# LayerNorm at a stage boundary of a two-layer hybrid step: the first four products on the raw input, mean and deviation applied on eviction

## The chip, the core and the metric

One core of one Trainium2 chip. The time is device microseconds from the first to the last instruction of one execution; a timed run takes the median of several executions. One further execution was taken by the hardware profiler, and all rows below are from it.

## What is computed

Two layers over 128 context and 256 latent tokens of width 1024. Each layer is FFN, mixer (low-rank attention beside a bidirectional RG-LRU), FFN, each closed by a LayerNorm of the sum with the input:

```
h = x * (1 + m[1]) + m[0]
x = layer_norm(ALPHA * x + 0.5 * m[2] * swiglu(h, w_ffn_up[0], w_ffn_down[0]), ...)
h = x * (1 + m[4]) + m[3]
x = layer_norm(ALPHA * x + m[5] * mixer(h), ...)
h = x * (1 + m[7]) + m[6]
x = layer_norm(ALPHA * x + 0.5 * m[8] * swiglu(h, w_ffn_up[1], w_ffn_down[1]), ...)
```

`swiglu` is silu(h Wg) * (h Wx) times W_down, with a hidden width of 2816. The nine vectors `m` of each layer are silu(cond) @ w_mod, one set for context tokens and one for latent tokens. The mixer's input projection makes four chunks of the recurrence's input (which first goes through a convolution over time, width 4), two of the key/value latent, the rotary key, three query chunks and four gate chunks.

## The kernel before

Activations lie transposed: X is 8 chunks of 128 features by 384 tokens in SBUF, fp32. Every product is done with three matmuls of a split in two halves: `piece` (L306) makes wh (a cast by ACT) and wl (a subtraction by DVE) of a weight block of 128 x 1024, `split_affine` (L275) makes hh and hl of the input, and `mm3` (L319) adds wh*hh + wh*hl + wl*hh into a PSUM tile. Four PSUM buffers ("acc") hold products, three split buffers hold pieces, three staging buffers of 1 MB hold weights that the SP queue loads, and three buffers "t1" of 128 x 384 hold short-lived activations.

A stage boundary is `next_input` (L453): the last chunk of the old stage is added to X (`Residual.add`, L347), the statistics are finished by single-column matmuls on PE (`moments`, L378), DVE subtracts the mean and multiplies by the reciprocal deviation, chunk by chunk (L400, L401; both vectors lie broadcast in PSUM), `split_affine` makes hh and hl of the chunk (ACT for hh; ACT for the fp32 copy of odd chunks and DVE for that of even ones; DVE for hl, L286), and POOL scales X for the next residual (L461). The first product of the new stage needs chunk 0 of hh and hl, and each product needs all eight chunks. There are five such boundaries; the last LayerNorm has its own class.

The vectors `m` are computed beside all this by a `Pump` of 64 steps, each with a load of w_mod (1 MB in one or two transfers) into one of three buffers. Vector steps run on DVE in the up stages of two FFNs; tensor steps are matmuls on PE (L238, tile "gm"). Where they stand is set by hand:

```
UP = [f for f in range(3, 21) if f % 3]
PLAN = ((UP, ()), (UP, ()), ((), ()), ((), ()))
NEXT_STEPS = (3, 3, 4, 3, 3)
MIX_STEPS = (14, 10)
```

NEXT_STEPS are run at the five boundaries, MIX_STEPS behind each mixer's attention. A framework puts each engine's instructions in a static order before the run: by program order among those that it reckons ready. So a step that stands late in the program fills holes in the work before it. Each engine then goes through its list in order.

Of the kernel before, what the change touches and what calls it, by code (L numbers as in the profile page):

```python
# [9 lines left out]
F32 = mybir.dt.float32  # L10
# [59 lines left out]
PLAN = ((UP, ()), (UP, ()), ((), ()), ((), ()))  # L70
NEXT_STEPS = (3, 3, 4, 3, 3)
MIX_STEPS = (14, 10)
# [3 lines left out]
def hybrid_step_kernel(ctx: ExitStack, tc: tile.TileContext, A):  # L76
# [182 lines left out]
    def h_tiles(name):  # L259
        hh = act.tile([P, KD, T], F32R, tag="hh", name=f"hh_{name}")  # L260
        hl = act.tile([P, KD, T], F32R, tag="hl", name=f"hl_{name}")
        return hh, hl
# [12 lines left out]
    def split_affine(hh, hl, c, G, B):  # L275
# [10 lines left out]
        nc.vector.tensor_tensor(hl[:, c, :], h32, hh[:, c, :].bitcast(F32), op=ALU.subtract)  # L286
# [37 lines left out]
    def product(ps, w, col, hh, hl, nk=KD):  # L324
        wh, wl = piece(w[:, :, col : col + P])
        for k in range(nk):
            mm3(ps, wh[:, k], wl[:, k], hh[:, k, :], hl[:, k, :], k == 0, k == nk - 1)
# [10 lines left out]
    class Residual:  # L338


        broadcast = True

        def __init__(self, name, gate):
            self.name, self.gate = name, gate
            self.sums = [tmp.tile([P, T], F32, tag=f"sum{i}", name=f"sum{i}_{name}", bufs=1) for i in range(2)]

        def add(self, c, ps):  # L347
            last = c == KD - 1
            with tc.high_priority(offset=CHAIN_AHEAD) if last else ExitStack():
                for r, (t0, t1) in enumerate(COND):  # L350
                    nc.vector.scalar_tensor_tensor(X[:, c, t0:t1], ps[:, t0:t1], self.gate[:, c, r : r + 1], X[:, c, t0:t1],  # L351
                                                   op0=ALU.mult, op1=ALU.add)
                sq = self.sums[1]
                if c > 0:
                    sq = tmp.tile([P, T], F32, tag="sq", name=f"sq_{self.name}_{c}", bufs=3)
                nc.scalar.activation(sq, X[:, c, :], AF.Square)
            if c == 0:
                return
# [19 lines left out]
        def moments(self):  # L378

            name = self.name  # L380
            with tc.high_priority(offset=CHAIN_AHEAD):
                self.columns(0, self.tail[0])
                self.columns(1, self.tail[1], stop=True)
                if self.broadcast:
                    nc.tensor.matmul(self.pm[:, :T], mean_w, self.tail[0], start=False, stop=True)
                mv = self.pt[:, :6].rearrange("p (a b) -> p a b", b=2)
                m2 = tmp.tile([P, 4], F32, tag="m2", name=f"m2_{name}")
                nc.scalar.activation(m2[:, :3], mv[:, :, 0], AF.Square)
                nc.vector.scalar_tensor_tensor(m2[:, :3], mv[:, :, 1], LN_EPS, m2[:, :3], op0=ALU.add, op1=ALU.subtract)
                rs = tmp.tile([P, 4], F32, tag="r4", name=f"r_{name}")  # L390
                nc.gpsimd.tensor_tensor(rs[:, :3], m2[:, :3], mhalf[:, :3], op=ALU.pow)
            return mv, rs

        def normalise(self):
            _, rs = self.moments()
            pm, pr = self.pm, misc_tile()
            for i in range(3):
                nc.tensor.matmul(pr[:, i * P : (i + 1) * P], rs[:, i : i + 1].to_broadcast([P, P]), ident, start=True, stop=True)
            for c in range(KD):
                nc.vector.tensor_tensor(X[:, c, :], X[:, c, :], pm[:, :T], op=ALU.subtract)  # L400
                nc.vector.tensor_tensor(X[:, c, :], X[:, c, :], pr[:, :T], op=ALU.mult)  # L401
                yield c

    class LastResidual(Residual):


        broadcast = False

        def __init__(self, name, gate):
# [16 lines left out]
        def finish(self, dsts):  # L426
            mv, rs = self.moments()
# [25 lines left out]
    def next_input(res, l, s, nl, nm, steps):  # L453
        pump.step(steps)
        pump.finish()
        G, B, ag = boundary_vectors(l, s, nl, nm)
        hh, hl = h_tiles(f"{nl}{nm}")
        for c in res.normalise():
            split_affine(hh, hl, c, G, B)
        for c in range(KD):  # L460
            nc.gpsimd.tensor_scalar(X[:, c, :], X[:, c, :], ag[:, 0, c : c + 1], ag[:, 1, c : c + 1],  # L461
                                    op0=ALU.mult, op1=ALU.add)
        return hh, hl


    def ffn(l, s, hh, hl, up_steps, down_steps, opened=(), residual=Residual):
        wu, wd = A["w_ffn_up"][l, s], A["w_ffn_down"][l, s]
        with tc.tile_pool(name=f"ffn{l}{s}", bufs=1) as fp:
# [3 lines left out]
            def gated(f, pg, px):  # L472
                a = tmp.tile([P, T], F32, tag="t1", bufs=3, name=f"a{l}{s}_{f}")
                nc.scalar.activation(a, pg[:, :T], AF.Silu)
                nc.vector.tensor_tensor(a, a, px[:, :T], op=ALU.mult)  # L475
# [6 lines left out]
            while f0 < NF:  # L482
                n = min(2, NF - f0)
                wg, wx = (load_rows(wu, 0, KD, o + P * f0, n * P) for o in (0, DFF))
                for i in range(n):
                    f = f0 + i
                    pg, px = acc_tile(), acc_tile()
                    product(pg[:, :T], wg, i * P, hh, hl)
                    product(px[:, :T], wx, i * P, hh, hl)
                    gated(f, pg, px)  # L490
# [10 lines left out]
            res = residual(f"f{l}{s}", gate)  # L501
# [34 lines left out]
    def mixer(l, hh, hl, steps):  # L536
        w_in = A["w_in"][l]
        with ExitStack() as es:
# [18 lines left out]
            for c in range(NLC):  # L557
                if c % 2 == 0:
                    w = load_rows(w_in, 0, KD, O_UX + c * P, 2 * P)
                ps = acc_tile()  # L560
                product(ps[:, :T], w, (c % 2) * P, hh, hl)
                conv(l, c, us[c], ps)
# [17 lines left out]
            for j in range(2):  # L580
                ps = acc_tile()
                product(ps[:, :T], w, j * P, hh, hl)
# [32 lines left out]
            product(ps[:, :T], w, 0, hh, hl)  # L615
# [15 lines left out]
            for j in range(3):  # L631
# [3 lines left out]
                product(ps[:, :T], w, (j % 2) * P, hh, hl)  # L635
# [15 lines left out]
            def gate_branch(c):  # L651
# [3 lines left out]
                product(ps[:, :T], w_g[0], (c % 2) * P, hh, hl)  # L655
# [75 lines left out]
            mh, ml = h_tiles(f"mix{l}")  # L731
            for c in range(NLC):
                nc.scalar.copy(mh[:, 4 + c, :], us[c])
                nc.vector.tensor_tensor(ml[:, 4 + c, :], us[c], mh[:, 4 + c, :].bitcast(F32), op=ALU.subtract)
# [4 lines left out]
            for hp in range(H // 2):  # L739
# [47 lines left out]
                nc.scalar.copy(mh[:, hp, :], ops[:, :T])  # L787
                nc.vector.tensor_tensor(ml[:, hp, :], ops[:, :T], mh[:, hp, :].bitcast(F32), op=ALU.subtract)
# [4 lines left out]
            res = Residual(f"m{l}", modv[l][:, 5])  # L793
            for j in range(KD // 2):
                w = load_rows(A["w_o"][l], 0, KD, 2 * P * j, 2 * P)
                for i in range(2):
                    ps = acc_tile()
                    wh, wl = piece(w[:, :, i * P : (i + 1) * P])
                    for n, k in enumerate((4, 5, 6, 7, 0, 1, 2, 3)):
                        mm3(ps[:, :T], wh[:, k], wl[:, k],  # L800
                            mh[:, k, :], ml[:, k, :], n == 0, n == KD - 1)
                    res.add(2 * j + i, ps)
        return res

    def conv(l, c, u, ps):
# [6 lines left out]
        nc.scalar.activation(u, ps[:, :T], AF.Identity, bias=vec["conv_b"][:, l * NLC + c : l * NLC + c + 1], scale=wk(2))  # L812
# [206 lines left out]
```

## Time and profile before

| | us |
|---|---|
| median of 3 timed runs | 1606.52 (1605.67 to 1615.58) |
| the profiled execution, its own time | 1607.12 |
| its span, first to last instruction | 1605.3 |
| PE busy | 1552.4 (97%) |
| DVE busy | 949.3 (59%) |
| ACT busy | 660.5 (41%) |
| POOL busy | 161.0 (10%) |

Matmuls overlap one another, so a busy PE can still be slow. In each stretch the count of product matmuls says how much of the stage's work was done. The profile shows the TensorE clock as a share of 2.4 GHz.

A row of the windows below has the window (us from the span's start), its length, then busy us and count of instructions of PE, weight loads, DVE, ACT and POOL in this order (with only one tile's instructions, the engines that touch it), then the granted clock, the busy share of the DMA engines and GB/s. Rows of groups by line have the line, engine, operation, out<-in with shapes and count, then busy us and the mean ns of one.

### The profile page before, as it was taken

The page shows a single profiled execution, that of the slowest core. Times are in us where ns is not written, and L with a number is a line of the kernel's source. Part 1 is how long each engine was busy: PE and PEld are TensorE (multiplying, and loading weights), DVE is VectorE, ACT ScalarE, POOL GpSimd, SP SyncE. Part 2 cuts the span into 40 slices and gives each one's busy share as a digit, 9 for nine tenths or more (in the row PEclk, how much of TensorE's full clock was granted, in tenths as well). Part 3 has the DMA queues.
Part 4 walks back from the last instruction along what each step waited for, and adds up shares of the span by engine and source line. Part 5 has one row for each costly group of instructions (what it writes and reads, how often), then busy time and mean ns, then how long its engine had stood idle before and what let it go on. Part 6 is the DMA issues. An engine that isn't in the chain of part 4 may idle for free.

```text
span 1605.3 us, 22927 instructions
## 1 busy us (share of the span) xinstructions
PE 1552.4 (97%) x9234; PEld 1448.7 (90%) x9234; DVE 949.3 (59%) x1568; ACT 660.5 (41%) x1068; POOL 161.0 (10%) x142
## 2 busy tenths in 40 slices
PE   6999999999999999999999999999999989999997
PEld 5899999987668899999989999997867789999996
DVE  3778754477986946863474444345788664444334
ACT  3533323268743533332253333234775444333321
POOL 0000002220004100001220000032000240000011
PEclk9999999999999999999999999999999989999998
DMA  8866563346644535563454343334565214433331
GB/s 295 278 215 203 173 202 133 116 151 209 226 166 157 184 117 199 184 203 119 134 183 150 106 137 119 128 107 157 152 193 197 79 53 131 142 121 128 121 118 40
DMA packets 214790, 249.93 MB, mean 156 GB/s; under 512 B 26394, under 2 KB 193308, under 8 KB 211612
## 3 DMA queue, kind: packets, MB, share of 16 engines
q1 hardware_dynamic: 214684, 248.47, 46.6%
q8 instruction: 72, 1.18, 0.3%
q14 instruction: 34, 0.28, 0.1%
HBM read 245.52 MB, written 1.88 MB: 154 GB/s over the span
## 4 chain that ended last, share of the span: by engine, by line
PE 87%; DVE 5%; issue 3%; DMA 2%; ACT 2%; POOL 1%; SPq 0%; DVEq 0%; POOLq 0%; ACTq 0%
PE acc L320 26%; PE acc L321 26%; PE acc L322 26%; PE gm L238 2%; DVE wl L316 1%; PE acc L753 1%; DMA wm<-in_w_mod_dram 1%; PE ms L375 1%; PE pv L786 1%; DMA ws<-in_w_ffn_up_dram 1%; PE ms L769 1%; ACT wh L315 0%; DVE hl L286 0%; POOL sum_f L361 0%; PE ms L320 0%
## 5 line engine op out<-in xcount | busy, mean ns | idle before, releaser
L315 ACT CAST wh<-ws 128x1024 fp32r<-128x1024 f32 (+1 forms) x332 | 336.2, 1014 | 779.4 <-PE acc L321 545.3
L316 DVE TENSOR_TENSOR wl<-ws,wh 128x1024 fp32r<-128x1024 f32 (+1 forms) x332 | 411.3, 1240 | 382.3 <-ACT wh L315 380.7
L320 PE MATMUL acc<-hh,wh 128*128 128x384 f32 x1280 | 428.6, 339 | 7.9 <-ACT hh L278 7.4
L322 PE MATMUL acc<-hh,wl 128*128 128x384 f32 x1280 | 431.0, 337 | 2.9 <-DVE wl L316 2.9
L321 PE MATMUL acc<-hl,wh 128*128 128x384 f32 x1280 | 431.1, 338 | 1.1 <-DVE hl L286 1.0
L320 PEld LDWEIGHTS acc<-hh,wh 128*128 128x128 f32 x1280 | 241.8, 190 | 15.7 <-ACT hh L278 9.2
L322 PEld LDWEIGHTS acc<-hh,wl 128*128 128x128 f32 x1280 | 241.9, 189 | 8.6 <-DVE wl L316 5.5
L321 PEld LDWEIGHTS acc<-hl,wh 128*128 128x128 f32 x1280 | 241.9, 189 | 8.5 <-DVE hl L286 4.9
L320 PE MATMUL acc<-gh,wh 128*128 128x384 f32 x704 | 236.9, 336 | 0.0
L321 PE MATMUL acc<-gl,wh 128*128 128x384 f32 x704 | 236.4, 336 | 0.0
L322 PE MATMUL acc<-gh,wl 128*128 128x384 f32 x704 | 236.1, 335 | 0.0
L320 PEld LDWEIGHTS acc<-gh,wh 128*128 128x128 f32 x704 | 132.2, 188 | 0.4 <-issue 0.4
L321 PEld LDWEIGHTS acc<-gl,wh 128*128 128x128 f32 x704 | 132.4, 188 | 0.0
L322 PEld LDWEIGHTS acc<-gh,wl 128*128 128x128 f32 x704 | 132.2, 188 | 0.0
L475 DVE TENSOR_TENSOR a<-a,acc 128x384 f32<-128x384 f32 x87 | 48.1, 553 | 123.1 <-PE acc L322 121.4
L252 DVE SCALAR_TENSOR_TENSOR gsum<-wm,sil,gsum 128x512 f32<-128x512 f32 x168 | 120.2, 764 | 0.0
L320 PE MATMUL acc<-hh_in,wh 128*128 128x384 f32 x336 | 111.6, 337 | 5.9 <-ACT hh_in L278 5.9
L321 PE MATMUL acc<-hl_in,wh 128*128 128x384 f32 x336 | 113.9, 339 | 0.0
L322 PE MATMUL acc<-hh_in,wl 128*128 128x384 f32 x336 | 113.9, 339 | 0.0
L360 POOL TENSOR_TENSOR sum_f<-X 128x384 f32<-128x384 f32 x4 | 5.1, 1281 | 841.2 <-DVE X L351 841.2
L320 PEld LDWEIGHTS acc<-hh_in,wh 128*128 128x128 f32 x336 | 62.7, 188 | 7.8 <-ACT hh_in L278 6.8
L238 PE MATMUL gm<-wm,sil 128*32 128x128 f32 (+2 forms) x640 | 62.2, 428 | 3.3 <-DVE G L915 1.2
(268 smaller groups left out, 1750.4 us busy)
## 6 DMA issues: line engine op xcount, KB each, us to landing
ws<-in_w_ffn_up_dram SPq DMA_DIRECT2D x84, 1024.0 KB, 5.1
wm<-in_w_mod_dram SPq DMA_DIRECT2D x56, 1024.0 KB, 6.6
ws<-in_w_ffn_down_dram SPq DMA_DIRECT2D x32, 1024.0 KB, 5.3
wm<-in_w_mod_dram SPq DMA_DIRECT2D x32, 512.0 KB, 4.5
ws<-in_w_ffn_down_dram SPq DMA_DIRECT2D x16, 768.0 KB, 4.5
ws<-in_w_in_dram SPq DMA_DIRECT2D x12, 1024.0 KB, 5.3
ws<-in_w_o_dram SPq DMA_DIRECT2D x8, 1024.0 KB
ws<-in_w_ffn_up_dram SPq DMA_DIRECT2D x8, 384.0 KB, 7.0
```

Of the source, the lines that this page charges most:

```text
L238: nc.tensor.matmul(self.ps[32 * g : 32 * g + 32, :n], lhsT, wv[:, g], start=self.fresh, stop=stop)
L252: nc.vector.scalar_tensor_tensor(self.sum[:, r], wv[:, kk], s, self.sum[:, r], op0=ALU.mult, op1=ALU.add)
L315: nc.scalar.copy(parts[0], src)
L316: nc.vector.tensor_tensor(parts[1], src, parts[0].bitcast(F32), op=ALU.subtract)
L320: nc.tensor.matmul(ps, wh, xh, start=start, stop=False)
L321: nc.tensor.matmul(ps, wh, xl, start=False, stop=False)
L322: nc.tensor.matmul(ps, wl, xh, start=False, stop=stop)
L375: nc.tensor.matmul(self.pt[:, 2 * i + j : 2 * i + j + 1], src[:, i * P : (i + 1) * P], mean_w[:, 0:1], start=False, stop=stop and i == T / ...
L475: nc.vector.tensor_tensor(a, a, px[:, :T], op=ALU.mult)
L753: nc.tensor.matmul(views[i], qT[hf][0:96, h % 4, q0 : q0 + P], kT[hf][0:96, h % 4, k0:k1], start=True, stop=True)
L769: nc.tensor.transpose(t0[:, (2 * j + i) * P : (2 * j + i + 1) * P], pr_[:, (0, 512)[i] + j * P : (0, 512)[i] + (j + 1) * P], ident)
L786: nc.tensor.matmul(o[:, P:T], v, pTs[e][:, (j - 1) * 256 : j * 256], start=(j == 1), stop=(j == 3))
```

## The change

The boundary is taken apart. While the old stage still runs, each finished chunk of X is scaled by G = (1 + m) * ln_g and split without LayerNorm (`split_raw`). The first four products of the new stage take these raw halves, and 4 extra columns behind the 384 tokens (-G and B, for context and latent), so that the products of the weights with -G and with B come out in columns 384 to 387 of the same PSUM tile. The four products run in two halves of four input chunks each (`by_half`). Statistics are put behind the second job of the first half, the broadcast deviation behind the fourth; mean and deviation are copied from PSUM to SBUF. On eviction `settle` adds mean times column and multiplies by the deviation. X is centred in `centre`; `normalise` does the multiplication, the split and the scaling on POOL for chunks 0 to 3 behind the first half, for chunks 4 to 7 behind the second. hh and hl are now one pair of tiles for the whole kernel. No pump steps stand at boundaries: 20 and 16 stand behind the two attentions, four in the up stage of the second layer's first FFN.

```diff
-PLAN = ((UP, ()), (UP, ()), ((), ()), ((), ()))
-NEXT_STEPS = (3, 3, 4, 3, 3)
-MIX_STEPS = (14, 10)
+PLAN = ((UP, ()), (UP, ()), ((6, 9, 12, 15), ()), ((), ()))
+MIX_STEPS = (20, 16)
+EXT = T + 4
+    def split_raw(c, G):
+        h32 = tmp.tile([P, T], F32, tag="t1", bufs=3, name=f"raw_{n_ps[0]}_{c}")
+        for r, (t0, t1) in enumerate(COND):
+            nc.scalar.activation(hh[:, c, t0:t1], X[:, c, t0:t1], AF.Copy, scale=G[:, c, r : r + 1])
+            nc.vector.tensor_scalar_mul(h32[:, t0:t1], X[:, c, t0:t1], G[:, c, r : r + 1])
+        nc.vector.tensor_tensor(hl[:, c, :T], h32, hh[:, c, :T].bitcast(F32), op=ALU.subtract)
+    def by_half(jobs, n, after):
+        for half in range(2):
+            k0 = half * HALF
+            parts = {}
+            for j, (ps, w, i) in enumerate(jobs):
+                if id(w) not in parts:
+                    parts[id(w)] = piece(w[:, k0 : k0 + HALF, :])
...
+                after(half, j)
...
+        def centre(self):
+            self.mean = tmp.tile([P, T], F32, tag="sum0", name=f"mean_{self.name}", bufs=1)
+            nc.scalar.copy(self.mean, self.pm[:, :T])
+            for c in range(KD):
+                nc.vector.tensor_tensor(X[:, c, :], X[:, c, :], self.pm[:, :T], op=ALU.subtract)
...
+        def normalise(self, c):
+            nc.vector.tensor_tensor(X[:, c, :], X[:, c, :], self.rstd, op=ALU.mult)
+            split_affine(c, self.G, self.B)
...
+        def settle(self, dst, ps, name):
+            v = tmp.tile([P, 4], F32, tag="ext", name=f"ext_{name}")
+            nc.vector.tensor_copy(v, ps[:, T:EXT])
+            for r, (t0, t1) in enumerate(COND):
+                nc.vector.scalar_tensor_tensor(dst[:, t0:t1], self.mean[:, t0:t1], v[:, r : r + 1], ps[:, t0:t1],
+                                               op0=ALU.mult, op1=ALU.add)
+            nc.vector.tensor_tensor(dst, dst, self.rstd, op=ALU.mult)
+            return v[:, 2:4]
+        def first(self, jobs, evict):
+            self.extend()
+            def after(half, j):
+                if half == 0:
+                    if j == 1:
+                        self.stats()
+                        self.centre()
+                    elif j == 3:
+                        self.deviation()
+                        for c in range(HALF):
+                            self.normalise(c)
+                else:
+                    evict(j)
+                    if j == 3:
+                        for c in range(HALF, KD):
+                            self.normalise(c)
+            by_half(jobs, EXT, after)
```

In an FFN the four jobs are the gate and the value product of hidden chunks 0 and 1, and hidden chunks 2 and 3 go through `by_half` too, with normalised input. Their eviction settles both products, then applies silu with the column for B as its bias. In the mixer the four jobs are the recurrence's input; each is settled into a t1 buffer, gets its bias from two activations, and goes through the convolution from there:

```diff
+            def settled(c):
+                u = tmp.tile([P, T], F32, tag="t1", bufs=3, name=f"ux{l}{c}")
+                b = prev.settle(u, ps[c], f"u{l}{c}")
+                for r, (t0, t1) in enumerate(COND):
+                    nc.scalar.activation(u[:, t0:t1], u[:, t0:t1], AF.Identity, bias=b[:, r : r + 1])
+                conv(l, c, us[c], u)
```

The last two products of the mixer's output projection are done together in two halves of the input, because hh is read there until the end; their chunks 0 to 5 are split raw only behind these matmuls.

## Rows read from the trace of the kernel before

**Rows 1.** busy time by window, steady FFN stretch and first attention

```profile
830.00:1090.00 260.00, 260.00 (x1501) 259.88 (x1501) 108.27 (x124) 87.66 (x118) 16.62 (x12) 1.00 0.38 125
366.00:490.00 124.00, 120.96 (x684) 87.69 (x683) 103.54 (x215) 79.54 (x159) 5.86 (x7) 1.00 0.61 206
```

**Rows 2.** the windows again, product matmuls alone (tile acc), five boundaries

```profile
315.30:345.30 30.00, 18.20 (x93) 16.72 (x93) 3.31 (x10) 2.01 (x3) 0.94 0.45 159
509.00:545.00 36.00, 22.43 (x109) 19.60 (x109) 1.34 (x4) 0.63 (x2) 0.95 0.31 102
808.80:838.80 30.00, 18.43 (x103) 17.27 (x102) 1.82 (x4) 0.96 (x2) 1.00 0.58 210
1096.00:1126.00 30.00, 16.51 (x84) 15.09 (x84) 2.77 (x8) 2.01 (x3) 0.94 0.44 156
1293.00:1330.00 37.00, 25.64 (x127) 23.84 (x126) 2.37 (x6) 0.87 (x2) 0.86 0.17 57
```

**Rows 3.** the windows again, the pump's instructions alone (tile gm)

```profile
315.30:345.30 30.00, 4.93 (x58) 1.92 (x58) 0.00 (x0) 0.94 0.45 159
509.00:545.00 36.00, 3.81 (x30) 0.84 (x30) 1.19 (x3) 0.95 0.31 102
808.80:838.80 30.00, 4.48 (x64) 2.00 (x64) 0.45 (x1) 1.00 0.58 210
1096.00:1126.00 30.00, 6.48 (x34) 1.15 (x34) 0.00 (x0) 0.94 0.44 156
```

**Rows 4.** the windows again, statistics alone (tile ms), third boundary

```profile
808.80:838.80 30.00, 5.40 (x36) 4.55 (x36) 8.24 (x17) 0.17 (x1) 1.00 0.58 210
```

**Rows 5.** timeline of PE, third and fifth boundary: start, us, [idle before]

```profile
813.83 2.79 PE L238 MATMUL gm<-wm,sil 128*32 128x256 f32 x46
...
1300.82 1.00 PE L375 MATMUL ms<-mean_w,X 128*128 128x1 f32 x6 [0.44 <-DVE X L351]
1304.53 1.65 PE L398 MATMUL ms<-ident,r_m 128*128 128x128 f32 x6 [1.40 <-POOL r_m L391]
1307.84 1.33 PE L320 MATMUL acc<-hh,wh 128*128 128x384 f32 x3 [1.67 <-ACT hh L278]
```

**Rows 6.** groups by line and shape: count, busy us, mean ns

```profile
L316 DVE TENSOR_TENSOR wl<-ws,wh 128x1024 fp32r<-128x1024 f32 x280 | 362.6, 1297 | 272.5 <-ACT wh L315 271.5
L351 DVE SCALAR_TENSOR_TENSOR X<-acc,gate,X 128x256 f32<-128x256 f32 x32 | 15.2, 474 | 0.0
L351 DVE SCALAR_TENSOR_TENSOR X<-acc,gate,X 128x128 f32<-128x128 f32 x32 | 11.2, 351 | 31.0 <-PE acc L322 29.7
L284 DVE TENSOR_SCALAR h<-X,G,B 128x256 f32<-128x256 f32 x20 | 9.0, 452 | 0.0
L284 DVE TENSOR_SCALAR h<-X,G,B 128x128 f32<-128x128 f32 x20 | 7.8, 389 | 0.0
L278 ACT ACTIVATE hh<-X,B,G 128x256 fp32r<-128x256 f32 x40 | 23.5, 587 | 0.0
L278 ACT ACTIVATE hh<-X,B,G 128x128 fp32r<-128x128 f32 x40 | 19.5, 488 | 21.0 <-DVE X L401 20.8
```

**Rows 7.** timeline of DVE and POOL, first boundary

```profile
313.29 2.08 DVE L316 TENSOR_TENSOR wl<-ws,wh 128x1024 fp32r<-128x1024 f32 x1 [0.16 <-ACT wh L315]
314.25 1.98 POOL L361 TENSOR_TENSOR sum_f<-sum_f,sq_f 128x384 f32<-128x384 f32 x1
...
320.70 2.40 DVE L400 TENSOR_TENSOR X<-X,ms 128x384 f32<-128x384 f32 x5
341.68 2.03 DVE L817 SCALAR_TENSOR_TENSOR uc<-acc,small,uc 128x126 f32<-128x126 f32 x6
```

**Rows 8.** one line's instructions: minimum, median and maximum ns

```profile
L401 DVE TENSOR_TENSOR X<-X,ms x40: 514/541/555, 324.0 to 1319.0; 128x384 f32<-128x384 f32 x40
...
L286 DVE TENSOR_TENSOR hl<-h,hh x40: 515/562/885, 326.1 to 1321.5; 128x384 fp32r<-128x384 f32 x40
```

**Rows 9.** the chain that ended last, first attention: start, us

```profile
435.53 4.37 DMA wm<-in_w_mod_dram
```

More of the change, by code (lines that the diff above doesn't have):

```diff
@@ L356, in add @@
                 nc.scalar.activation(sq, X[:, c, :], AF.Square)
+                if c == KD - 1 and self.broadcast:
+                    split_raw(c, self.G)
+            if c < KD - 1 and self.early:
+                split_raw(c, self.G)
             if c == 0:
@@ L376, in columns, with stats @@
                                  start=False, stop=stop and i == T // P - 1)
-        def moments(self):
+        def stats(self):
             name = self.name
[L381 to L392, printed above, removed]
@@ L394, in normalise @@
-        def normalise(self):
-            _, rs = self.moments()
-            pm, pr = self.pm, misc_tile()
-            for i in range(3):
[L398 to L402, printed above, removed]
+            if self.broadcast:
+                nc.tensor.matmul(self.pm[:, :T], mean_w, self.tail[0], start=False, stop=True)
@@ L451, in boundary_vectors, with ffn @@
         return G, B, ag
[L453 to L466, printed above, removed]
+    def ffn(l, s, prev, up_steps, down_steps, after, opened=()):
         wu, wd = A["w_ffn_up"][l, s], A["w_ffn_down"][l, s]
@@ L484, in ffn, with evict @@
                 wg, wx = (load_rows(wu, 0, KD, o + P * f0, n * P) for o in (0, DFF))
+                if prev is not None and f0 < 4:
+                    ps = [acc_tile() for _ in range(4)]
+                    jobs = [(ps[2 * i + e], w, i) for i in range(2) for e, w in enumerate((wg, wx))]
+                    def evict(j, f0=f0, ps=ps):
+                        if j % 2:
+                            gated(f0 + j // 2, ps[j - 1], ps[j], prev if f0 == 0 else None)
+                    if f0 == 0:
+                        prev.first(jobs, evict)
+                    else:
+                        by_half(jobs, T, lambda half, j: evict(j) if half else None)
                 for i in range(n):
                     f = f0 + i
[L487 to L490, printed above, removed]
+                    if prev is None or f0 >= 4:
+                        pg, px = acc_tile(), acc_tile()
+                        product(pg[:, :T], wg, i * P)
+                        product(px[:, :T], wx, i * P)
+                        gated(f, pg, px)
                     if f - 2 in up_steps:
@@ L500, in ffn @@
             nc.vector.tensor_scalar_mul(gate, modv[l][:, m], 0.5)
-            res = residual(f"f{l}{s}", gate)
+            res = (Residual if after else LastResidual)(f"f{l}{s}", gate, after)
             for j in range(KD // 2):
@@ L534, in token_scale, with mixer @@
         return pr
-    def mixer(l, hh, hl, steps):
+    def mixer(l, prev, steps, after):
         w_in = A["w_in"][l]
@@ L810, in wk @@
             return vec["conv_w"][:, i : i + 1]
[L812 removed]
+        nc.scalar.activation(u, x, AF.Identity, bias=vec["conv_b"][:, l * NLC + c : l * NLC + c + 1], scale=wk(2))
         for k in (0, 1, 3):
```

149 lines of the change are left out of this document (96 added, 53 removed).

## Prediction

> **What bounds the kernel now.** First I read the page: PE is busy 97% of the span, DVE 59%, ACT 41%, so the question is where PE is slow rather than where it is idle. The windows give the scale: in a steady FFN stretch PE starts 1501 matmuls in 260 us, one each 0.1732 us, at full clock [rows 1]. I call that the price of a product matmul, and ask of each boundary how much of its time is not product matmuls at that price [rows 2]:
>
> - first (FFN to mixer, layer 0): 30 us less 93 x 0.1732 = 16.1 leaves 13.9
> - second (mixer to FFN): 36 less 109 x 0.1732 = 18.9 leaves 17.1
> - third (FFN to FFN, next layer): 30 less 17.8 leaves 12.2
> - fourth (FFN to mixer, layer 1): 30 less 14.5 leaves 15.5
> - fifth (mixer to the last FFN): 37 less 22.0 leaves 15.0
>
> That is 73.7 us, 4.6% of the span. It has three parts. Statistics and broadcast matmuls take PE 5.4 us at a boundary [rows 4], 27.0 in all; they stay. The pump's steps take 4.9, 3.8, 4.5, 6.5 and nothing [rows 3], 19.7 in all: they fill holes here and would cost something elsewhere. The rest is waiting and slow clock: 3.6, 7.9, 2.3, 3.6 and 9.6, together 27.0 us. The timeline of PE shows it at the fifth boundary, which has no pump work: 1.40 us until POOL has the deviation, 1.67 until ACT has the first hh, then three matmuls in 1.33 us [rows 5]; the window's granted clock is 0.86 [rows 2], a mixture of the two levels 1.2 and 2.4 GHz, where the third boundary keeps 1.00.
>
> So 27.0 + 19.7 = 46.7 us would be the gain if no wait were left and every pump step were hidden elsewhere. What the change gets of it hangs on DVE, which does most of what is added.
>
> **The change part by part: FFN boundaries (second, third, fifth).** PE now has work from the first moment: 48 matmuls of the first half, 48 of the second, and 48 of the first half of the next four products, which need normalised chunks 0 to 3 alone. That is 144 x 0.1732 = 24.9, with statistics 30.3 us before a chunk of 4 to 7 is wanted. In that time DVE must do, at mean durations of [rows 6] and medians of [rows 8]: the last chunk's residual 0.82 (0.47 + 0.35) and raw split 1.50 (scale 0.84; subtraction between 0.56 and 0.885, I take 0.66); eight subtractions of the mean and eight multiplications at 0.54, 8.6; scales of four even chunks 3.4; eight subtractions for hl 5.3; four settles at 1.52 (two operations with a PSUM operand at 0.82 as the residual's, a multiplication 0.54, a copy of four columns at some 0.16), 6.1; the gate's two operations and split for two hidden chunks 2.7; six weight pieces at 1.30, 7.8. The sum is 36.2. Back to back DVE is a tenth faster than single durations say (five subtractions in 2.40, 0.48 each [rows 7]), 32.6. So DVE is 2 to 6 us late at the end of its list. The chunks come one by one, and four products can use each, so I take 2 us of wait, between 0 and 6. ACT has four activations for odd and two for even chunks, 12.9 us at [rows 6], plus casts and silu: its list is shorter.
>
> POOL sums chunk 6 just before the statistics, and beside a weight piece its addition took 1.98 and the piece 2.08 against a mean of 1.30 [rows 6, 7]. The raw split of chunk 6 now lies in that stretch too: 0 to 1.2 us for PE, I take 1. The four extra columns are 96 matmuls x 4/384 of 0.173, 0.2 us a boundary. Together 3.2 us of wait where there are 7.9, 2.3 and 9.6.
>
> The raw splits of chunks 0 to 5 or 6 in the down stage cost nothing: DVE is busy 108 of 260 us there and ACT 88 [rows 1]; in the output projection they lie beside the last 48 matmuls (8.3 us; six splits at 1.50 are 9.0 on DVE) and half of them is wanted at once, the rest 8 us later. If that cover fails, it costs up to 2 us at the second and fifth boundaries. The boundary's small vectors and the extra columns' split are a few instructions over 16 elements, issued while the old stage still runs; uncovered they would be under 1 us.
>
> Gain: second 7.9 + 3.8 - 3.2 = 8.5, third 2.3 + 4.5 - 3.2 = 3.6, fifth 9.6 - 3.2 = 6.4; 18.5 in all, with pump steps counted as gone.
>
> **Mixer boundaries (first, fourth).** Here the cover is shorter: 96 matmuls, 16.8 us with the columns, and 5.4 of statistics, then only first halves of the next two products (4.2), 26.4 us. DVE's list has the convolutions: six operations a chunk, 2.03 us [rows 7], 8.1 in all, and they stand in program order ahead of the normalisation of chunks 4 to 7, as do the settles. Without the gate and with four pieces the sum is 0.8 + 1.5 + 8.6 + 3.4 + 5.3 + 6.1 + 8.1 + 5.2 = 39.0, back to back 35. PE then waits 8.6; I take 8 (4 where a third product runs ahead and the order is kind, 18 in the rival below). The boundary then has 5.4 + 0.2 + 8 = 13.6 us outside products against 13.9 and 15.5 now, 2.2 us better. But of the 4.9 + 6.5 of pump work in these windows only some 3 us each fit the new hole; 5.4 go into the attention, and half of it shows there. Sum: 0.
>
> **The pump's steps that move.** Four go into the up stage of the second layer's first FFN, where PE has no hole: 64 instructions at 2.79/46 [rows 5] = 3.9 us lost. The second boundary's 30 instructions are 16 that belong to a vector group and stay (0.6) and 14 that go to the attention. There DVE is busy 103.5 of 124 us and PE starts one matmul in 0.18 us [rows 1], so DVE leaves PE holes, but not many. I take 1.5, between 0 and 3. Each moved step also issues 1 MB on the SP queue, ahead of weights for the attention's products, and a matmul of the pump that waits for it holds PE: the chain has one such wait of 4.37 us at 435.5 [rows 9].
>
> **Sum.** 18.5 - 3.9 - 0.6 - 1.5 + 0 = 12.5 us. The profiled execution took 1607.1 (span 1605.3, 1.8 around it), 0.6 above the median; from the median the forecast is 1594, 0.8% faster.
>
> **The rivals.**
>
> *The order is kind.* If DVE slips the second half's multiplications into its waits, the FFN boundaries wait 1.2 us and the mixers 4: 3 x 2 + 2 x 4 = 14 more, 1580. For it: the order before already interleaves chunks closely, and DVE waits for PE or ACT now and then. Against: the program order puts settles and convolutions first.
>
> *The moved pump work shows in full.* Nine steps' worth more in the attentions at 0.97 us each (16 instructions of [rows 5]), 8.7, less 4.2 counted, and one more wait of 4.4 for a load: 1594 + 9 = 1603.
>
> *The multiplication meets POOL.* The deviation moves from PSUM to SBUF. Over 40 instructions the multiplication with PSUM stays between 514 and 555 ns, though POOL scales X beside it; the subtraction for hl, with both inputs in SBUF, runs from 515 to 885 [rows 8]. So each of eight multiplications may cost 0.33 us more: 2.6 us a boundary on an engine that is late, 13 in all, 1607. Against: most of the 40 subtractions are near the median of 562. The Trainium skill has this as a rule (SBUF — State Buffer, "Who interferes with whom"): a VectorE instruction with two SBUF inputs contends with a GpSimd instruction that reads SBUF, one with a single SBUF input doesn't. By that rule all eight can be held up, and the trace agrees with both halves of it.
>
> *Slower: the mixers' settled inputs block the list.* Each holds one of the three t1 buffers from its settle to the end of its convolution: 1.5 + 1.1 (bias on ACT) + 0.6 (the convolution's first step there) + 2.0 = 5.2 us, and the normalisation of chunks 4 to 7 needs the same buffers. If ACT and DVE alternate without overlap, four inputs end 21 us after the first at 16, chunk 7 follows near 46, and PE waits up to 18 us at each of two boundaries: 20 more than in the sum, 1614, and with the two rivals above 1631. It decides against the change once these two waits pass 14 us each. For it: nothing in the present order holds t1 so long. Against: ACT is the less loaded engine.
>
> *It doesn't do what it says:* if PE's static order puts the statistics ahead of the raw products, the old wait of some 3 us per boundary stays; 1606. Unlikely, since the raw products are ready first.
>
> **How the numbers follow.** Forecast 0.40, kind order 0.25, pump work 0.13, multiplication 0.10, settled inputs 0.09, the last 0.03. A measurement here tells 1% from no change, 16 us; the three runs span 0.6%. Faster by over 1% is below 1590.5: the kind order and a quarter of the forecast's case (its own range is 1587 to 1601), 0.35. Slower by over 1% is above 1622.6: half of the settled inputs and a little for what I don't see, 0.08. The rest, 0.57, is within 1%. The range goes from 1576 (kind order with a hidden pump) to 1610 and leaves out the settled inputs and the far ends.
>
> **What would show it.** Right: at the FFN boundaries the time outside products falls to about 8.6 us (plus what pump work is there), the clock stays at 1.00, and PE's first raw product follows the old stage's last within 3 us; in the mixer windows PE waits for the hl or hh of chunk 4 with DVE busy throughout, some 8 us. The up stage of the second layer's first FFN grows by 4 us. Wrong: a PE wait in the middle of an FFN boundary for a settle or a weight piece; mixers' waits well under 4 or over 14 us; multiplications with a mean near 0.8; an attention that grows by more than 5 us, with PE waiting for a load of w_mod. The prediction falls if DVE's list isn't what PE waits for.

## The result and the profile after

The changed kernel takes 1620.4 us against 1606.6 before, ratio 1.0084 (95% interval 1.0064 to 1.0105). The forecast was 1594, with a range from 1576 to 1610: it went the other way, 26 us from the forecast. The profiled run took 1621.7 (span 1619.9).

At the boundaries much of what I had said would show does: PE goes on with raw products and the time outside products falls. The windows of [rows 2] and [rows 3] again, each at the same distance from its stage's start: product matmuls (tile acc), then the pump (tile gm). Columns: stretch, its length, busy and count of PE, PEld, DVE, (ACT), granted clock, DMA share, GB/s.

```profile
318.70:348.70 30.00, 20.88 (x111) 19.29 (x110) 3.29 (x11) 0.00 (x0) 1.00 0.27 82
516.30:552.30 36.00, 30.16 (x163) 28.06 (x161) 3.46 (x12) 0.00 (x0) 1.00 0.26 85
816.00:846.00 30.00, 24.48 (x132) 22.72 (x131) 4.24 (x14) 0.00 (x0) 1.00 0.33 108
1104.40:1134.40 30.00, 20.80 (x111) 19.29 (x110) 3.30 (x11) 0.00 (x0) 1.00 0.27 84
1301.20:1338.20 37.00, 29.87 (x144) 27.67 (x144) 2.39 (x8) 0.00 (x0) 0.86 0.23 78
...
318.70:348.70 30.00, 3.41 (x48) 1.56 (x48) 0.00 (x0) 1.00 0.27 82
516.30:552.30 36.00, 0.41 (x2) 0.14 (x2) 0.00 (x0) 1.00 0.26 85
816.00:846.00 30.00, 1.69 (x18) 0.56 (x18) 0.00 (x0) 1.00 0.33 108
1104.40:1134.40 30.00, 3.82 (x24) 0.79 (x24) 0.00 (x0) 1.00 0.27 84
```

At 0.1732 us a product, as in the prediction, the time outside products is 10.8, 7.8, 7.1, 10.8 and 12.1, together 48.6 where it was 73.7: 25.1 us less, 10.4 of it pump work that left (19.7 to 9.3). The 30 us behind the first window give a part of it back: 137 matmuls of all kinds at a clock of 0.89, where before (second fence) 164 started.

```profile
348.70:378.70 30.00, 25.59 (x137) 19.82 (x138) 23.22 (x52) 24.07 (x44) 6.63 (x5) 0.89 0.66 239
```

```profile
345.30:375.30 30.00, 29.20 (x164) 25.95 (x162) 22.91 (x46) 22.72 (x35) 1.56 (x3) 1.00 0.43 132
```

And 100 us in the middle of the last up stage, far from any boundary, hold nine products fewer than before, with PE busy throughout at full clock. After, then before; the last row has the products alone in 85 us of the last down stage before, for use below:

```profile
1360.00:1460.00 100.00, 100.00 (x570) 99.87 (x569) 40.91 (x48) 33.94 (x48) 0.00 (x0) 1.00 0.39 127
```

```profile
1347.00:1447.00 100.00, 100.00 (x579) 100.00 (x578) 41.84 (x49) 34.83 (x49) 0.00 (x0) 1.00 0.39 127
...
1500.00:1585.00 85.00, 84.47 (x475) 82.25 (x474) 4.45 (x12) 0.00 (x0) 1.00 0.28 90
```

100 us by 570 is 175.4 ns a product, by 579 172.7. No boundary explains that. 5280 of the 7728 product matmuls read hh or hl (counted in both traces); 2.2 ns each, the difference of their mean start-to-start times (those under 0.3 us: 177.05 at 384 columns, 174.86 before), is 11.6 us, nearly the whole loss.

The stages tell where the rest is: us from the last product of one to the last of the next (an up stage to the first product of its down stage; the opening stage from 19.0 us of the span), worked out from the traces. The down stages are the same in all of these, 91.3 to 91.5, the last 94 to 95. The kernels e2 to e18 are those of the experiments below.

```
                           opening mixer 0  FFN 01  FFN 10 mixer 1  FFN 11
before                       204.7   201.0   201.1   195.8   204.2   195.2
after                        208.1   204.9   201.0   196.8   204.0   201.9
before, 256 bytes more (e2)  206.8   201.8   203.2   199.3   202.2   197.4
before, light pump (e16)     203.5   205.4   200.2   197.2   208.4   195.3
pitch 388, band, raw (e9)    206.1   204.1   204.4   196.7   202.5   197.0
pitch 388, raw at FFNs (e10) 205.7   201.1   209.8   196.6   199.5   198.5
pitch 448, raw (e13)         204.1   203.5   204.6   194.7   209.5   199.9
the same, light pump (e15)   203.1   202.6   204.4   194.2   202.9   198.3
pitch 448, raw at FFNs (e18) 204.5   199.5   208.3   194.7   194.5   198.3
pitch 448, plain (e14)       203.9   200.0   200.7   195.0   194.5   195.8
pitch 384, plain (e17)       206.2   200.5   200.6   195.0   201.8   195.7
```

### The profile page after: what moved, and what is told of

It is laid out like the page before. It is cut to its first block, busy times and chain, and to the rows that moved or that the text cites. A ratio compares the mean times of both kernels' runs of the same rounds, so it can differ in the third digit from the quotient of the medians.

```text
span 1619.9 us, 23332 instructions
## 1 busy us (share of the span) xinstructions
PE 1560.1 (96%) x9234; PEld 1461.2 (90%) x9234; DVE 1030.1 (64%) x1784; ACT 702.7 (43%) x1190; POOL 182.6 (11%) x142
## 4 chain that ended last, share of the span: by engine, by line
PE 84%; DVE 8%; ACT 2%; DMA 2%; issue 2%; POOL 1%; SPq 0%; DVEq 0%; ACTq 0%; POOLq 0%
PE acc L326 25%; PE acc L328 25%; PE acc L327 25%; PE gm L238 2%; PE acc L845 1%; DMA wm<-in_w_mod_dram 1%; DVE wl L322 1%; DVE uc L923 1%; PE ms L403 1%; DMA ws<-in_w_ffn_up_dram 1%; PE pv L878 1%; DVE tr L980 1%; DVE hl L284 1%; ACT wh L321 1%; DVE X L443 1%
## 5 line engine op out<-in xcount | busy, mean ns | idle before, releaser
L327 PE MATMUL acc<-hl,wh 128*128 128x384 f32 (+1 forms) x1744 | 592.4, 340 | 9.9 <-DVE hl L284 9.9
L326 PE MATMUL acc<-hh,wh 128*128 128x384 f32 (+1 forms) x1744 | 593.8, 344 | 8.2 <-ACT hh L276 7.5
L328 PE MATMUL acc<-hh,wl 128*128 128x384 f32 (+1 forms) x1744 | 597.1, 342 | 3.0 <-DVE wl L322 2.9
L326 PEld LDWEIGHTS acc<-hh,wh 128*128 128x128 f32 x1744 | 329.2, 189 | 22.8 <-ACT hh L276 9.7
L327 PEld LDWEIGHTS acc<-hl,wh 128*128 128x128 f32 x1744 | 331.1, 190 | 16.6 <-DVE hl L284 13.3
L328 PEld LDWEIGHTS acc<-hh,wl 128*128 128x128 f32 x1744 | 330.4, 189 | 7.9 <-DVE wl L322 5.0
L445 POOL TENSOR_SCALAR X<-X,ag 128x384 f32<-128x384 f32 x40 | 57.1, 1435 | 93.9 <-DVE h L282 68.9
L388 POOL TENSOR_TENSOR sum_f<-sum_f,X 128x384 f32<-128x384 f32 x20 | 30.7, 1537 | 200.9 <-DVE X L375 200.7
L551 ACT CAST gh<-a 128x384 fp32r<-128x384 f32 x88 | 44.7, 509 | 13.3 <-DVE a L542 9.2
L552 DVE TENSOR_TENSOR gl<-a,gh 128x384 fp32r<-128x384 f32 x88 | 48.6, 552 | 1.2 <-ACT gh L551 1.2
```

The source lines that it names most:

```text
L326: nc.tensor.matmul(ps, wh, xh, start=start, stop=False)
L327: nc.tensor.matmul(ps, wh, xl, start=False, stop=False)
L328: nc.tensor.matmul(ps, wl, xh, start=False, stop=stop)
L388: nc.gpsimd.tensor_tensor(self.sums[0], X[:, 0, :] if c == 1 else self.sums[0], X[:, c, :], op=ALU.add)
L445: nc.gpsimd.tensor_scalar(X[:, c, :], X[:, c, :], self.ag[:, 0, c : c + 1], self.ag[:, 1, c : c + 1], op0=ALU.mult, op1=ALU.add)
L551: nc.scalar.copy(gh[:, f, :], a)
```

## The experiments

**Is it the pitch of the rows?** The chunks of hh and hl stand 388 floats apart instead of 384. Four kernels, the first two made from the one before (here and below the edits are shortened):

```diff
e1: - act.tile([P, KD, T])      + act.tile([P, KD, T + 4])[:, :, :T]
e2: - act.tile([P, KD, T])      + act.tile([P, KD * (T + 4)]), pitch T as before
e3, e4 (from after): - act.tile([P, KD, EXT])  + [P, KD, 400], [P, KD, 392]; nat, gate: bufs=1
```

> The kernel before, unchanged but for the two tiles of split rows (hh, hl), whose chunks stand 388 floats apart (1552 bytes) instead of 384 (1536); the same 384 columns are read. Theory (the row pitch makes each product that reads them start later): the trace after has these products at a mean of 177.05 ns against 174.86 before, 2.2 ns by 5280 products = +11.6 us, so about 1618. Rival (the loss lies in the change's own instructions around the boundaries and in the attention): 1606.5, as before.

> The kernel before, with the same 256 bytes more in all for the two tiles as in the run with 388 floats, but the chunks inside 384 floats apart as before, so that only the tiles that follow in SBUF are moved. Theory (pitch of the rows that are read): 1606.5, as before. Rival (the tiles behind them, the split weights above all, are moved to worse addresses): about 1618.

> The changed kernel with its chunks 400 floats apart (1600 bytes, a multiple of 64) instead of 388; columns and instructions as in the changed kernel; two small tiles (nat, gate) have one buffer in place of two to make room. Theory (pitch): the 4800 products of 384 columns and 480 of 388 fall back, 10.5 + 1 to 2.4 us less than 1620.4, so 1607 to 1610. Rival (boundaries and attention): 1620, unchanged.

> As the run with 400 floats, with 392 (1568 bytes, a multiple of 32 and not of 64). If a multiple of 32 bytes is enough: 1607 to 1610. If it takes 64: 1613 to 1620. If the pitch is not the cause: 1620.

Measured: 1620.2 (ratio 1.0074, 1.0047 to 1.0101), 1619.2 (1.0073, 1.0051 to 1.0095), 1626.0 and 1619.1. The second is the surprise: the rows keep their pitch, only hl and what lies behind it move, and 12 us are lost all the same. The same stretch of its last up stage:

```profile
1355.00:1455.00 100.00, 100.00 (x571) 100.00 (x570) 40.56 (x48) 34.78 (x48) 0.00 (x0) 1.00 0.39 127
```

So the theory falls as stated: it is a matter of place, not of pitch, and wider pitches (e3, e4) don't mend it.

**Place against what?** In the kernel before, X, hh and hl have 12288 bytes a partition each and the staging tiles 24576, all multiples of 256: every row of hh and hl starts where the split weights (wh, wl, rows of 512 bytes) start, modulo 256. In e2 hl is moved by 128 bytes against hh, and the weights by 256. These kernels take the two apart (e7 also has one buffer for nat and gate in place of two, 576 bytes in all, to make room):

```diff
- act.tile([P, KD, T])
+ act.tile([P, KD * T + n])   # hh, hl: n = 0, 64 (e5); 64, 0 (e6); 0, 128 (e7); 0, 32 (e8) floats
```

> The kernel before, pitch 384, with 256 spare bytes behind hl: hh and hl stay where they were to each other, and the split weights (wh, wl) stand 256 bytes further from both. The run with room for 388 floats had moved hl by 128 bytes against hh and the weights by 256, and had 12 us more. Theory A (the distance from the rows to the split weights that are loaded beside them, modulo 512, sets the start-to-start time): slow again, 175 ns or more a product in the last up stage against 173.3, about 1618. Theory B (the distance between hh and hl): as before, 173.3 ns and 1606.5.

> The kernel before with 256 spare bytes between hh and hl: hl and the weights keep their distance, hh is 256 bytes further from both. Theory A: the products of hl (one in three) are as before and those of hh slow, so some 174.5 ns in the last up stage, 1610 to 1616. Theory B: slow, about 1618, if 256 bytes between hh and hl is as bad as 128.

> The kernel before with 512 spare bytes behind hl (the small tile nat has one buffer in place of two): the weights are 512 bytes further. Theory A with a modulus of 512: as before, 173.3 ns in the last up stage and 1606.5. If the modulus is larger: slow, about 1618. Theory B: as before. The rows of gh come to stand 128 bytes below the weights modulo 512, where they stood 64 below; by theory A the down stages could get slower, by B not.

> The kernel before with 128 spare bytes behind hl: the weights are 128 bytes further from hh and hl. Theory A: between before and the run with 256 bytes, 1606.5 to 1618, which tells where the loss begins. Theory B: as before, 1606.5.

Measured, one run each: 1606.8, 1604.6, 1612.4, 1624.7, beside 1611.0 for the kernel before. In 100 us of the last up stage there are 578, 579, 578 and 570 matmuls. By these counts moves by 256 or 512 bytes cost nothing; 128 costs it in full. e8:

```profile
1365.00:1465.00 100.00, 100.00 (x570) 100.00 (x570) 41.69 (x48) 34.53 (x48) 0.00 (x0) 1.00 0.39 125
```

e7 holds a second case. Its hh rows are fast, but by the addresses of the built program gh, the rows of the down stages, has come to stand 128 bytes from the weights modulo 256, where it stood 64 below. Now the down stage is slow, 470 products where 475 were (second row, products alone):

```profile
1352.00:1452.00 100.00, 100.00 (x578) 100.00 (x578) 41.85 (x50) 34.81 (x48) 0.00 (x0) 1.00 0.39 127
...
1505.00:1590.00 85.00, 84.47 (x470) 82.23 (x469) 4.46 (x12) 0.00 (x0) 1.00 0.28 90
```

Three findings of the traces don't fit a rule by the distance between row and weights alone. In e2 only hl is 128 bytes from the weights, a third of the products, and the loss is as large as in e8: an hl product takes 178.2 ns to the next start, the others 173.9 and 174.5, where in e8 all three kinds take 176 (means of distances under 0.23 us, worked out from the traces; 173.5 before). In e8 gh moves together with the weights, yet two of its four down stages grew, to 93.2 and 92.2 us from 91.5. And in the changed kernel hh, whose rows stand 0 to 112 bytes from the weights, loses more (176.4 ns) than hl, which stands 128 to 240 from them (174.4). So a place 128 bytes off costs time in each of these runs, but how much, and whether the distance or a tile's own place decides, stays open.

**With a pitch of 388 or 448, and the raw path undone in parts.** At 1552 bytes a row moves 16 bytes against the weights from chunk to chunk. First all rows were put within 64 bytes of the weights (e9), then parts of the change undone on that; nat and gate have one buffer in these four:

```diff
e9:  + 32 floats behind hh, 48 behind hl
e10, e11: + if not prev.raw: stats, normalise and split c = 0..7; by_half(jobs, T, evict)
          # raw = False ahead of the mixers (e10), of the FFNs (e11)
e12: - self.load(1)   + self.load(WM_AHEAD)   # in Pump.step
```

> The changed kernel, pitch 388, with spare bytes behind hh (128) and hl (192), so that a row of chunk k starts 64 bytes below the split weights modulo 256 at k = 0 and 48 above at k = 7, in hh and in hl (in the changed kernel hh stood at 0 to 112, hl at 128 to 240); nat and gate have one buffer in place of two for the room. Theory A, as the runs on the kernel before have left it (128 bytes modulo 256 between rows and weights cost 2.2 to 2.7 ns a product; 0 and 64 below cost nothing): products of 384 columns at 173.5 to 174 ns in the last up stage, 8 to 11 us less than the changed kernel, 1609 to 1612. Rival (only rows that all start at the same place modulo 256 are fast, so that a pitch of 1552 bytes loses wherever it is put): 175.8 ns and 1620.

> The aligned changed kernel in which the two boundaries ahead of a mixer take normalised input again (statistics with priority, all eight chunks normalised and split, then the four products, whose accumulators the convolution reads); the three boundaries ahead of an FFN stay raw, the pump plan stays. If the raw path is worth nothing at a mixer, as forecast: as the aligned kernel, within 3 us. If the wait that follows there (3 us on hl in each mixer) and the fuller VectorE cost more than the wait that it removes: 3 to 8 us faster than the aligned kernel. If the raw path does pay at a mixer: 2 to 5 us slower.

> The aligned changed kernel in which the three boundaries ahead of an FFN take normalised input again; those ahead of a mixer stay raw. The forecast put 18.5 us on these three: 18 us slower than the aligned kernel. By the trace after, whose time outside products in the three falls by some 7 us beyond the pump work that left: 4 to 8 us slower.

> The aligned changed kernel with three pieces of the modulation weights asked for ahead in every pump step in place of one. In the changed kernel TensorE waits 5.7 us for these DMAs (four times), against 0.5 us in the attention before. If the wait is a late request: 3 to 6 us faster than the aligned kernel. If the DMA queues or the buffers set it: within 1 us of it.

Measured: 1618.1, 1620.1, 1618.2, 1626.3. A narrow band is not enough (572 matmuls in the 100 us); theory A's form with a band falls. Undoing either half of the raw path changed no time that these runs can tell, though the forecast had put 18.5 us on the FFN half. The stage table says more of e10: with normalised input each mixer stage is 3.0 us shorter than in e9, and FFN 01 is 5.4 longer, FFN 11 1.5. Asking for the pump's weights earlier cost 8 us: a miss, both theories wrong.

The next four have 448 floats from chunk to chunk, 1792 bytes = 7 x 256, so that all rows stand right (e15 and e16 leave out most products of the 16 steps that the change moves, so their vectors lack part of their sums):

```diff
e13: - act.tile([P, KD, EXT])  + act.tile([P, KD, 448]);  nat: tag="sq";  ti: bufs=1
e14: e13, raw = False at all five boundaries
e15 (from e13), e16 (from before), in add_tensor:
  + if self.done - 8 in MOVED and not self.fresh and not stop: return
```

> The changed kernel with its chunks 448 floats apart (1792 bytes, 7 times 256), so that every row of hh and hl starts at the same place modulo 256 as the split weights; for the room, the small tile nat shares the buffers of sq and the tile ti of the scan has one buffer in place of two. The aligned kernel with pitch 388 was not faster (175.55 ns in the last up stage), so a narrow band around the weights' place is not enough. Theory A2 (rows and weights must keep one distance modulo 256 from chunk to chunk, and not 128): 173.3 ns in the last up stage and 11 us less than the changed kernel, 1607 to 1610. Rival (something else in the change makes the products start later): 175.5 ns and 1618 to 1620.

> As the run with 448 floats, with normalised input at all five boundaries (statistics with priority, eight chunks normalised and split, then the four products); the pump plan and the early vectors of the changed kernel stay. It gives the worth of the raw path alone, with products at the same rate. Forecast: 18.5 us at the FFN boundaries and nothing at the mixers, so 18 us slower than with 448 floats. By the pitch 388 pair (FFN boundaries undone: 1618.2 against 1618.1; mixers undone: 1620.1): within 3 us of it.

> As the run with 448 floats, but 11.5 of the 16 moved pump steps' TensorE products are left out (of each affected group only the first and the last product of the sum are kept, so four modulation vectors lack part of their sum); their weights are still loaded. If the moved work shows in full in the attention and the up stage: 12 to 15 us less than with 448 floats (19.7 us by 11.5/16 = 14). If the attention hides it, as the forecast half assumed (3.9 + 0.6 + 1.5 us for the 16): 3 to 6 us less.

> The kernel before with the same 11.5 steps' TensorE products left out, where they stand at the boundaries. If the pump work at the boundaries is only filling (the waits would be there without it): 0 to 5 us less than before. If it shows in full: 12 to 15 us less, 1592 to 1595.

Measured: 1622.8, 1594.5 (ratio 0.9927, 0.9906 to 0.9947), 1610.1, 1621.4. In the last two 136 of the pump's 832 instructions are gone, and its time on PE falls by 15.9 us from e13 and by 14.2 from before (windows of tile gm over the whole span). In the stretch far from the boundaries e13 has the old rate back,

```profile
1361.00:1461.00 100.00, 100.00 (x579) 100.00 (x578) 41.99 (x50) 35.20 (x49) 0.00 (x0) 1.00 0.39 127
```

and is no faster than the changed kernel: its mixer 1 stage grew to 209.5 us. e14, the same without the raw path, is 28 us faster than e13 and beats both kernels. Part of the distance is clock (span and mean granted clock, e13, then e14):

```profile
core 0: 1619.9 us, clock 0.978
```

```profile
core 0: 1593.6 us, clock 0.988
```

0.022 of 1619.9 against 0.012 of 1593.6 is 35.6 against 19.1, so by this estimate, which takes PE as busy throughout, 16.5 of the 26 us between the spans. Most of it lies in mixer 1, 0.94 in e13 and 1.00 in e14:

```profile
1100.20:1309.70 209.50, 197.85 (x1070) 158.98 (x1069) 163.73 (x339) 127.64 (x252) 33.94 (x28) 0.94 0.43 144
```

```profile
1093.00:1287.40 194.40, 190.09 (x1067) 150.60 (x1066) 149.76 (x302) 118.54 (x226) 32.23 (x28) 1.00 0.48 156
```

There the clock fell at a wait. In e13's second mixer (timeline of PE: start, us, idle before) three products that started 0.17 us apart before the waits start 0.32 apart after them, at the lower level (granted clock 0.50 from 1139.3 to 1145.9):

```profile
1136.56 0.34 PE L328 MATMUL acc<-hh,wl 128*128 128x384 f32 x1
1136.73 0.34 PE L327 MATMUL acc<-hl,wh 128*128 128x384 f32 x1
1136.91 0.34 PE L328 MATMUL acc<-hh,wl 128*128 128x384 f32 x1
1137.81 0.61 PE L326 MATMUL acc<-hh,wh 128*128 128x384 f32 x2 [0.57 <-ACT hh L276]
1140.15 0.69 PE L327 MATMUL acc<-hl,wh 128*128 128x384 f32 x1 [1.73 <-DVE hl L284]
1140.64 0.52 PE L328 MATMUL acc<-hh,wl 128*128 128x384 f32 x1
1140.96 0.52 PE L326 MATMUL acc<-hh,wh 128*128 128x384 f32 x1
1141.28 0.52 PE L327 MATMUL acc<-hl,wh 128*128 128x384 f32 x1
```

Two last runs: e17 is the plain version at a pitch of 384 with the changed kernel's buffers, e18 is e13 with raw = False ahead of the mixers alone.

> Everything of the change but the raw path, with 384 floats from chunk to chunk again, no extra columns, and the tiles nat and ti as in the changed kernel. The run with 448 floats and plain boundaries took 1594.45. If it is the rest of the change (pump steps away from the boundaries, the vectors of the next input made early, the four first products by halves) that gained those 12 us: 1592 to 1597 again. If the 448 floats or the shared buffers did it: back towards 1606.

> As the run with 448 floats (1622.8), with normalised input ahead of the two mixers and raw input ahead of the three FFNs, where the forecast put its gain of 18.5 us. Forecast: 18 us faster than with normalised input everywhere (1594.45), so 1576. Theory C (the raw path costs at both kinds of boundary, by what waits for the normalised split afterwards and by the clock that falls there): between 1594 and 1622; by the runs with pitch 388, in which the two kinds gave 5 to 7 us of loss each in the FFN and mixer stages of the first layer, 1600 to 1612.

Measured: 1602.0 (0.9975, 0.9961 to 0.9990) and 1604.1 (0.9977, 0.9960 to 0.9994). Against e14 the raw path at the FFNs, as e18 has it, costs 7.6 us in FFN 01, nothing in FFN 10 and 2.5 in FFN 11 (stage table). Most of the 7.6 can be read from e18's timeline: POOL, then DVE, then PE, second boundary.

```profile
515.03 1.32 POOL L391 TENSOR_TENSOR sum_m<-sum_m,sq_m 128x384 f32<-128x384 f32 x1
522.01 1.00 POOL L390 TENSOR_TENSOR sum_m<-sum_m,X 128x384 f32<-128x384 f32 x1 [5.66 <-DVE X L377]
...
514.41 1.07 DVE L293 TENSOR_TENSOR hl<-raw,hh 128x384 fp32r<-128x384 f32 x1 [0.22 <-ACT hh L291]
515.52 0.92 DVE L292 TENSOR_SCALAR raw<-X,G 128x128 f32<-128x128 f32 x1
...
519.73 1.49 DVE L293 TENSOR_TENSOR hl<-raw,hh 128x384 fp32r<-128x384 f32 x3
521.13 1.38 DVE L377 SCALAR_TENSOR_TENSOR X<-acc,modv,X 128x128 f32<-128x128 f32 x4
...
516.96 0.44 PE L328 MATMUL acc<-hl,wh 128*128 128x388 f32 x1 [0.62 <-DVE hl L293]
523.06 1.23 PE L405 MATMUL ms<-mean_w,sum_m 128*128 128x1 f32 x5 [5.66 <-POOL sum_m L390]
```

DVE works the raw splits of chunks 0 to 5 first; the residual of chunk 6, which was written behind them, runs at 521.13. POOL waits 5.66 us for it, PE 5.66 for POOL's sum, and the raw products stand behind these statistics in PE's order. In e14, without raw splits, POOL adds that chunk 6.9 us earlier:

```profile
515.15 1.00 POOL L390 TENSOR_TENSOR sum_m<-sum_m,X 128x384 f32<-128x384 f32 x1
```

A kernel with that residual ahead of the splits was not tried, so that their order is the cause is read from the trace and not shown by a run.

## Why the prediction was wrong

**The step that failed first: "The four extra columns are 96 matmuls x 4/384 of 0.173, 0.2 us a boundary".** It prices the reading of the columns and leaves out what they do to the tiles' place: 388 floats move hl by 128 bytes and every chunk by 16 against the weights, modulo 256. Every product on hh and hl pays, 480 with the columns and 4800 without. Priced at 0.9 us, it is 11.6 by the traces; the same move alone costs 12.4 to 13.4 (e1, e2). No rival held it, so the range could not. It is not the whole: with the rows right e13 is as slow as the changed kernel, and 28.3 us hang on the raw path (e13 against e14).

**"Gain: ... 18.5 in all" at the FFN boundaries.** The windows fell as forecast in two of three (7.8 and 7.1 where 8.6 was to be; the fifth 12.1 with its clock still 0.86), but a window of 30 us isn't the stage. At the fast rate the raw path loses about 10 us over the three stages (e18 against e14, stage sum 7.6 - 0.3 + 2.5). The sum also has 8.3 us of "pump steps counted as gone" (3.8 and 4.5); FFN 01 with its 3.8 gone and normalised input (e14) is 0.4 us shorter than before. The term that a trace shows to be mis-sized is "The raw splits of chunks 0 to 5 or 6 ... cost nothing", with "up to 2 us" if the cover fails: it counted DVE's time and not its order. PE's wait for the sum at the second boundary is 5.7 us in e18, 3.1 in e13 and 0.8 in e14; in the changed kernel it is 1.9 there and 1.9 at the fifth:

```profile
PE acc L327 <- DVE hl L284: 9.9, 8, 1.8
PE acc L326 <- ACT hh L276: 7.5, 8, 3.1
PE gm L238 <- DMA wm<-in_w_mod_dram: 5.7, 4, 1.6
PE ms L403 <- POOL sum_m L388: 3.7, 2, 1.9
```

These waits don't fill the distance from 18.5 gained to 10 lost; the rest is not assigned.

**The mixers, "Sum: 0".** I had PE wait 8 us for chunk 4's split; it waits 1.8 and 1.3 for hl in the first mixer, 0.9 and 1.7 in the second (5.8 of the 9.9 above). The loss came otherwise: the clock falls at these waits (0.89 in the 30 us shown). At the fast rate the two mixer stages are 3.5 and 15.0 us longer with the raw path (e13 against e14), and of the 15.0 some 12.6 is clock (0.06 of 209.5, an estimate). At pitch 388 the same edit gave no time (e9, e10), because what it wins in the mixers is lost behind them: PE's wait for the sum ahead of FFN 01 rises from 1.9 to 5.7 us, as it does from 3.1 to 5.7 at pitch 448 (e13, e18).

```profile
PE ms L406 <- POOL sum_m L391: 7.6, 2, 5.7
```

So the worth of one half of the raw path depends on the other. Why the residual comes later behind a mixer with normalised input is not shown.

**The pump's steps, 6.0 us lost.** The rival "shows in full" comes near in the sum: without 11.5 of the 16 steps' products, e13 gets 12.6 us faster (e15). By stages it holds in mixer 1 alone: 6.6 us for 6.8 of products, with the clock up from 0.94 to 0.97. Mixer 0 is 0.9 us shorter for 6.2 less, and the up stage on which the forecast put 3.9 (FFN 10) 0.5 for 3.4; the rest of the gain lies where none of these products stood. My reading that the steps "fill holes here" was right as well, and worth more than I gave it: taken away from the boundaries before, the kernel gets 14.5 us slower (e16), with a clock of 0.979 and a wait of 3.3 us for a query in each mixer that was not there; the two mixer stages grew by 4.4 and 4.2. Yet with the raw path gone as well, the moved plan gains (e14, e17). Which part of what is left gains (steps, early vectors, halves) stays open. e14 has 194.5 us in mixer 1 and e17 201.8, at a clock of 1.00 and 0.97: in e17 PE waits 3.3 us for a query there, in e14 it doesn't. What makes that query late is not shown.

**The multiplication meets POOL: fell.** With both inputs in SBUF its 24 instructions after the FFNs run from 537 to 558 ns (the 16 after the mixers from 540 to 552). It is POOL that got slower: its scaling of X rose from a mean of 906 to 1435 ns, beside all that DVE does there, the multiplications among it.

```profile
L443 DVE TENSOR_TENSOR X<-X,rstd_f x24: 537/551/558, 333.1 to 1140.5; 128x384 f32<-128x384 f32 x24
```

```profile
L445 POOL TENSOR_SCALAR X<-X,ag 128x384 f32<-128x384 f32 x40 | 57.1, 1435 | 93.9 <-DVE h L282 68.9
```

The Trainium skill's rule is that the two lock each other out and that the order of issue decides which of them waits (SBUF — State Buffer, "Who interferes with whom"). The rows agree that one of them pays; the order of issue is not in them.

**A term read too small.** The 5.4 us of statistics was read at the third boundary and taken for all five; the five windows have 5.4 to 6.4, 28.9 in all in place of 27.0.

**The account.** Before to e14, the change without the raw path, with its rows right and other buffers for nat and ti: -12.4 (at a pitch of 384 with the changed kernel's buffers -4.3, e17). The raw path on e14: +28.3 (e13). From there to the changed kernel, with smaller pitch, slow products and other buffers: -2.4. In the stage table four stages lose 9.5 us together on that last step, and FFN 01 (204.6 to 201.0) and mixer 1 (209.5 to 204.0) win back 9.1, with the clock up from 0.97 to 1.00 and from 0.94 to 0.97. That e14 takes 1594, as forecast for the change, is chance: it is the kernel without the step from which the forecast took its gain.

## What to carry to other kernels

When an edit changes the size of a tile that TensorE reads, look at the start-to-start time of a product in a stretch far from the edit, and if it changed, compare where the moving rows and the weights stand (here modulo 256 bytes) before you look for waits. A window around the edit shows what moved out of it, not what came back behind it: compare whole stages, and their clock. Before you put work into an idle engine's queue, ask what small instruction is written behind it and who waits for that.

## What the runs showed of the hardware

At a granted clock of 1.00 a product of 128x128 weights on 384 fp32r columns started every 172.7 ns (100 us by 579) where the moving row and the weights start at the same place modulo 256 bytes, also after moves by 256 and 512 (579, 578 and 578 in e6, e5 and e7). At 128 bytes it is 175.4 (570 in e8), and 175 where the distance changes from row to row (572 in e9). Another pair of tiles agrees: 85 us of the last down stage hold 475 products on gh at 64 bytes below the weights (before) and 470 at 128 (e7). e2 and the down stages of e8 show that the distance alone doesn't give the size of the loss. The Trainium skill gives TensorE a read port for the moving operand and one for weights, independent of each other (SBUF — State Buffer, "Who interferes with whom"). By that rule the distance between the two would cost nothing; the runs differ by 12 us, and they decide. What the reads meet in, or whether it is these two reads that meet, isn't shown.
